# First factor of the state-space powers read by VectorE from PSUM, copied there by TensorE identity products

## The chip, the core and the metric

The program runs on one core of one Trainium2 chip. Its engines work side by side, each through its own instructions in order: TensorE (PE in the profile, with its weight loads as PEld), VectorE (DVE), ScalarE (ACT), GpSimd (POOL), and SyncE (SP), which here only issues DMA transfers. The metric is device time in microseconds (us) for one execution; lower is better.

## The reference

A trunk of two layers over 256 tokens of width 2048. Layer 0 is stick-breaking attention and a squared-ReLU MLP, layer 1 is an S5 state-space mixer with a gated unit and the same kind of MLP. What matters here are the S5 parameters, 128 groups of 64 complex states with 16 channels each:

```
mag = exp(lr * dt);  ar = mag * cos(li * dt);  ai = mag * sin(li * dt)
bbr = fr * b_re - fi * b_im;  bbi = fr * b_im + fi * b_re
h(t) = a * h(t-1) + bb * u(t)          # complex, one scan per state
y    = Re(c * h)                       # c_re, c_im
x    = x + g2 * ((relu(h @ w1) ** 2) @ w2)   # the MLP, in both layers
```

The kernel works in blocks of four time steps, so it needs b and c multiplied by the first three powers of a. These products depend on parameters alone; the change touches how the products of b are formed.

## The kernel before, in words

**The matrix products.** All large products are split in two parts for accuracy. `weights` (L124) loads a tile of 512 KB through SP (tile `w`), ScalarE rounds it to `wh` (L130), and VectorE writes the remainder `wl = w - wh` (L132). `cols_tile` then gives TensorE 24 products for it (L159 with `wl`, L160 and L161 with `wh`). `w`, `wh` and `wl` have three buffers each, so VectorE can be at most three tiles ahead of TensorE.

**The modulation vectors.** Beside these, VectorE accumulates the conditioning products (L348, L350) from tiles `adaw`, 512 KB each in four buffers, also loaded through SP. A tile of `adaw` gives two instructions. How many of them go beside one `w` tile is set by a rate in the code.

**The state-space parameters.** During the first MLP, `s5_tables` (L810) plans for each of eight groups `gi` of parameters: `s5_raws` at tick 30 + 22 gi, `s5_powers` 9 ticks later, and `s5_turns` (phase tables, GpSimd) twice; a tick is one tile of `w`. `s5_raws` issues DMAs on GpSimd's queue: b into `W` (L875), c into `C` (L879). `W` and `C` have one buffer. In `s5_powers`, TensorE transposes `C` (L895), ScalarE copies it out (L898), GpSimd forms the products of c in 13 instructions (L902 to L916), and VectorE forms the products of b in six (L920 to L925):

```
        e0, e1 = (Ec[:, c, 0:1].to_broadcast([P, 3, 8, 16]) for c in range(2))
        v.tensor_tensor(u1, e0, ar, op=OP.mult)
        v.tensor_tensor(u2, e1, ai, op=OP.mult)
        v.tensor_tensor(Ec[:, 0, 1:], u1, u2, op=OP.subtract)
        v.tensor_tensor(u1, e1, ar, op=OP.mult)
        v.tensor_tensor(u2, e0, ai, op=OP.mult)
        v.tensor_tensor(Ec[:, 1, 1:], u1, u2, op=OP.add)
        g_.dma_start(self.pw[gi], W)
```

`Ec` is the half of `W` into which the DMA of L875 has put b; `powers` holds a, a², a³. At the end GpSimd's queue sends `W` to DRAM (L926), and the next group's `s5_raws` may then overwrite it.

**What sets the order.** TensorE and GpSimd keep the order in which the code is written (`manual_schedule` in `run`). The order of VectorE, ScalarE and SP is made by a scheduler, which places an instruction where it expects its operands to be there. On the chip every engine then keeps that order, whatever is late. PSUM tiles for small results come from `mp`, four buffers in turn.

Of the kernel before, what the change touches and what calls it, by code (L numbers as in the profile page):

```python
# [16 lines left out]
P = 128  # L17
# [39 lines left out]
class Trunk:  # L57
# [824 lines left out]
    def s5_powers(self, sp, gi):  # L882
        nc, s5 = self.nc, self.s5
        v, g_ = nc.vector, nc.gpsimd
        half = lambda t, a: t[64 * a:64 * a + 64]
        qs = slice(8 * gi, 8 * gi + 8)
        bc = lambda t: t[:, qs][:, :, None].to_broadcast([P, 8, 16])
        W, C = self.raw
        Ec, Cc = W[:, 0], W[:, 1]
        CT = sp.tile([P, 2, 8, 16], F32, name="CT", bufs=1)  # L890
        pt = self.mp()
        for c in range(2):
            for b in range(2):
                o = (2 * c + b) * P
                nc.tensor.transpose(pt[:, o:o + P], C[:, c, b].rearrange("p a b -> p (a b)"), self.ident)  # L895
        for a in range(2):
            src = half(pt, a).rearrange("p (c q a e) -> p c q a e", c=2, a=2, e=16)[:, :, :, a]
            nc.scalar.activation(half(CT, a), src, AF.Copy)  # L898
        t1 = sp.tile([P, 3, 8, 16], F32, name="t1", bufs=1)
        t2 = sp.tile([P, 3, 8, 16], F32, name="t2", bufs=1)  # L900
        cr, ci, fr, fi = CT[:, 0], CT[:, 1], bc(s5["fr"]), bc(s5["fi"])
        g_.tensor_tensor(t1[:, 0], cr, fr, op=OP.mult)  # L902
        g_.tensor_tensor(t2[:, 0], ci, fi, op=OP.mult)
        g_.tensor_tensor(Cc[:, 0, 0], t1[:, 0], t2[:, 0], op=OP.subtract)
        g_.tensor_tensor(t1[:, 0], cr, fi, op=OP.mult)
        g_.tensor_tensor(t2[:, 0], ci, fr, op=OP.mult)
        g_.tensor_tensor(t1[:, 0], t1[:, 0], t2[:, 0], op=OP.add)
        g_.tensor_scalar(Cc[:, 1, 0], t1[:, 0], -1.0, None, op0=OP.mult)
        ar, ai = (s5[n][:, :, qs][:, :, :, None].to_broadcast([P, 3, 8, 16]) for n in ("ar", "ai"))
        c0, c1 = (Cc[:, c, 0:1].to_broadcast([P, 3, 8, 16]) for c in range(2))  # L910
        g_.tensor_tensor(t1, c0, ar, op=OP.mult)
        g_.tensor_tensor(t2, c1, ai, op=OP.mult)
        g_.tensor_tensor(Cc[:, 0, 1:], t1, t2, op=OP.add)
        g_.tensor_tensor(t1, c1, ar, op=OP.mult)
        g_.tensor_tensor(t2, c0, ai, op=OP.mult)
        g_.tensor_tensor(Cc[:, 1, 1:], t1, t2, op=OP.subtract)  # L916
        u1 = sp.tile([P, 3, 8, 16], F32, name="w1", bufs=1)
        u2 = sp.tile([P, 3, 8, 16], F32, name="w2", bufs=1)
        e0, e1 = (Ec[:, c, 0:1].to_broadcast([P, 3, 8, 16]) for c in range(2))
        v.tensor_tensor(u1, e0, ar, op=OP.mult)  # L920
        v.tensor_tensor(u2, e1, ai, op=OP.mult)
        v.tensor_tensor(Ec[:, 0, 1:], u1, u2, op=OP.subtract)
# [4 lines that stand above are left out]
# [300 lines left out]
```

## Time and profile before

| | us |
|---|---|
| median of 3 runs (lowest to highest) | 2525.38 (2521.66 to 2526.85) |
| the profiled execution, its own time | 2524.86 |
| span of that execution in the trace | 2523.1 |
| PE busy | 2376.2 |
| DVE busy | 1833.1 |
| ACT busy | 1208.5 |
| POOL busy | 292.2 |

The time holds 1.8 us more than the span, for what lies before the first and after the last instruction. Busy times overlap between engines and say nothing of what waits for what; for that the trace is read. The first MLP runs from about 500 to about 1390 us of the span.

### The profile page before, as it was taken

The numbers are of one execution on the slowest core, as the hardware profiler recorded it, in microseconds if no ns is written. First come the engines' busy times: TensorE is split into PE (matmuls) and PEld (weight loads), VectorE is DVE, ScalarE is ACT, GpSimd is POOL, SyncE is SP. The second block draws the span as 40 slices with busy tenths as digits, with TensorE's granted clock in tenths as the row PEclk, the third lists the DMA queues.
The fourth block names the chain that finished last, engine by engine and source line by source line (L and its number), as shares of the span: only waits on it lengthen the run. The fifth ranks groups of instructions, "written<-read, shape, count | busy, mean of one in ns | idle before, by whom it ended". The sixth has DMA issues, their size and how long they took to land.

```text
span 2523.1 us, 48416 instructions
## 1 busy us (share of the span) xinstructions
PE 2376.2 (94%) x19843; PEld 2236.4 (89%) x19843; DVE 1833.1 (73%) x2479; ACT 1208.5 (48%) x1806; POOL 292.2 (12%) x340
## 2 busy tenths in 40 slices
PE   7998999999887789788999999999999999999998
PEld 4776789899887789788999999999999999999998
DVE  5789999999787759756977897698654555554543
ACT  4534875355333334333555677444543543543543
POOL 0000100001315532345300000000000000000000
PEclk9999999999998899899999999999999999999999
DMA  9888899999987758866986884599655655655654
GB/s 335 302 300 297 282 315 316 338 308 306 310 269 266 259 180 295 271 220 205 315 291 223 289 298 139 171 325 325 218 180 184 184 184 184 184 184 184 184 188 138
DMA packets 479250, 627.28 MB, mean 249 GB/s; under 512 B 19858, under 2 KB 350004, under 8 KB 476724
## 3 DMA queue, kind: packets, MB, share of 16 engines
q1 hardware_dynamic: 474432, 606.16, 72.9%
q0 software_dynamic: 3968, 17.83, 2.2%
q8 instruction: 155, 2.54, 0.4%
q14 instruction: 67, 0.55, 0.1%
q10 hardware_dynamic: 628, 0.21, 0.0%
HBM read 607.34 MB, written 16.78 MB: 247 GB/s over the span
## 4 chain that ended last, share of the span: by engine, by line
PE 42%; DVE 5%; DMA 4%; issue 2%; ACT 1%; SPq 0%; DVEq 0%; ACTq 0%
PE acc L159 13%; PE acc L161 12%; PE acc L160 12%; DMA adaw<-in_ada_w 3%; DVE wl L132 2%; DVE adsums L350 1%; PE mp L997 1%; PE mp L1022 1%; PE mp L982 1%; PE mp L959 1%; PE mp L952 0%; DVE xT L418 0%; DVE adacc L350 0%; PE mp L967 0%; DMA W<-pw 0%
## 5 line engine op out<-in xcount | busy, mean ns | idle before, releaser
L130 ACT ACTIVATE wh<-w 128x1024 fp32r<-128x1024 f32 x736 | 777.3, 1058 | 1067.0 <-PE acc L161 617.0
L132 DVE TENSOR_TENSOR wl<-w,wh 128x1024 fp32r<-128x1024 f32 x736 | 918.6, 1249 | 417.6 <-ACT wh L130 417.2
L159 PE MATMUL acc<-hH,wl 128*128 128x258 f32 (+1 forms) x2816 | 811.9, 288 | 57.5 <-DVE wl L132 56.7
L161 PE MATMUL acc<-hH,wh 128*128 128x258 f32 (+1 forms) x2816 | 802.2, 285 | 0.0
L160 PE MATMUL acc<-hL,wh 128*128 128x258 f32 (+1 forms) x2816 | 800.9, 284 | 0.1
L159 PE MATMUL acc<-aH,wl 128*128 128x256 f32 x2048 | 583.0, 285 | 45.2 <-DVE wl L132 45.1
L159 PEld LDWEIGHTS acc<-hH,wl 128*128 128x128 f32 x2816 | 538.7, 191 | 74.2 <-DVE wl L132 55.4
L160 PE MATMUL acc<-aL,wh 128*128 128x256 f32 x2048 | 579.1, 283 | 0.0
L161 PE MATMUL acc<-aH,wh 128*128 128x256 f32 x2048 | 579.0, 283 | 0.0
L160 PEld LDWEIGHTS acc<-hL,wh 128*128 128x128 f32 x2816 | 539.6, 192 | 0.3 <-DVE hL L122 0.3
L161 PEld LDWEIGHTS acc<-hH,wh 128*128 128x128 f32 x2816 | 538.0, 191 | 0.0
L159 PEld LDWEIGHTS acc<-aH,wl 128*128 128x128 f32 x2048 | 388.5, 190 | 52.6 <-DVE wl L132 50.7
L160 PEld LDWEIGHTS acc<-aL,wh 128*128 128x128 f32 x2048 | 388.6, 190 | 0.0
L161 PEld LDWEIGHTS acc<-aH,wh 128*128 128x128 f32 x2048 | 388.5, 190 | 0.0
L350 DVE SCALAR_TENSOR_TENSOR adacc<-adaw,cond,adacc 128x512 f32<-128x512 f32 x390 | 296.7, 762 | 22.2 <-DMA adaw<-in_ada_w 18.4
L350 DVE SCALAR_TENSOR_TENSOR adsums<-adaw,cond,adsums 128x512 f32<-128x512 f32 x270 | 213.5, 792 | 22.1 <-DMA adaw<-in_ada_w 19.1
L145 PE MATMUL acc<-wh,hL 128*128 128x512 f32 x384 | 157.8, 411 | 5.8 <-ACT wh L130 3.1
L146 PE MATMUL acc<-wl,hH 128*128 128x512 f32 x384 | 154.4, 402 | 4.8 <-DVE wl L132 4.7
L147 PE MATMUL acc<-wh,hH 128*128 128x512 f32 x384 | 153.5, 400 | 0.0
L145 PEld LDWEIGHTS acc<-wh,hL 128*128 128x128 f32 x384 | 73.7, 192 | 32.4 <-issue 12.8
L146 PEld LDWEIGHTS acc<-wl,hH 128*128 128x128 f32 x384 | 73.6, 192 | 23.3 <-DVE wl L132 8.2
L147 PEld LDWEIGHTS acc<-wh,hH 128*128 128x128 f32 x384 | 73.4, 191 | 17.1
(292 smaller groups left out, 2107.9 us busy)
## 6 DMA issues: line engine op xcount, KB each, us to landing
w<-in_mlp_w SPq DMA_DIRECT2D x512, 512.0 KB, 3.8
adaw<-in_ada_w SPq DMA_DIRECT2D x384, 512.0 KB, 5.8
w<-in_sb_w_in SPq DMA_DIRECT2D x96, 512.0 KB, 5.0
w<-in_s_w_glu SPq DMA_DIRECT2D x64, 512.0 KB, 4.6
w<-in_sb_w_out SPq DMA_DIRECT2D x32, 512.0 KB, 6.0
w<-in_s_w_in SPq DMA_DIRECT2D x32, 512.0 KB, 4.9
pw<-W POOLq DMA_DIRECT2D x8, 1024.0 KB, 6.2
W<-pw SPq DMA_DIRECT2D x8, 1024.0 KB, 6.9
```

Source lines behind the costliest of these rows:

```text
L130: nc.scalar.activation(h, w, AF.Copy)
L132: nc.vector.tensor_tensor(l, w, h.bitcast(F32), op=OP.subtract)
L145: nc.tensor.matmul(o, aL(kb)[:, s], H[:, kk], start=(kb == k0), stop=False)
L146: nc.tensor.matmul(o, aH(kb)[:, s], L[:, kk], start=False, stop=False)
L147: nc.tensor.matmul(o, aH(kb)[:, s], H[:, kk], start=False, stop=(kb == k1 - 1))
L159: nc.tensor.matmul(o, L[:, kk, s], aH(kb), start=(kb == k0), stop=False)
L160: nc.tensor.matmul(o, H[:, kk, s], aL(kb), start=False, stop=False)
L161: nc.tensor.matmul(o, H[:, kk, s], aH(kb), start=False, stop=(kb == k1 - 1))
L350: nc.vector.scalar_tensor_tensor(acc, wt[:, kk], c, acc, op0=OP.mult, op1=OP.add)
L959: nc.tensor.transpose(pe[:, q * P:q * P + P], E[:, c, q].rearrange("p j a e -> p (j a e)"), self.ident)
L982: nc.tensor.matmul(pi[32 * j:32 * j + 32, 65 * q:65 * q + 65], self.ident[:, 32 * q:32 * q + 32], uw[:, 4 - j:4 - j + 257:4], start=True, ...
L997: nc.tensor.matmul(pv[:, 256 * c + 64 * q:256 * c + 64 * q + 64], VL[:, c, q], imc[:, q, 0:64], start=True, stop=True)
```

## The change

Before the transposes of `C`, TensorE multiplies the two halves of b (`Ec[:, c, 0]`, 128 x 128 each) by the identity into a tile `eb` of the pool `mp`. The four multiplications of VectorE then read their first factor from `eb` in PSUM, not from `W` in SBUF. Nothing else is edited; the two sums (L922, L925) and GpSimd's work are as before.

```
         CT = sp.tile([P, 2, 8, 16], F32, name="CT", bufs=1)
+        eb = self.mp()
+        for c in range(2):
+            nc.tensor.matmul(eb[:, c * P:c * P + P], self.ident, Ec[:, c, 0].rearrange("p q e -> p (q e)"), start=True, stop=True)
+        eb = eb[:, :2 * P].rearrange("p (c q e) -> p c q e", c=2, q=8)
         pt = self.mp()
...
-        e0, e1 = (Ec[:, c, 0:1].to_broadcast([P, 3, 8, 16]) for c in range(2))
+        e0, e1 = (eb[:, c, None].to_broadcast([P, 3, 8, 16]) for c in range(2))
         v.tensor_tensor(u1, e0, ar, op=OP.mult)
```

Lines after the insertion are numbered four higher: L895 becomes L899, L920 to L926 become L924 to L930.

The order of instructions shows what this moves. On TensorE, at the second of the eight groups (gi = 1), before; a number behind a name is that of the buffer's use, and the row of L895 stands between the products of two weight tiles, of which `wl_7758` is the second:

```order
L161 MATMUL acc_7691<-hH_4644,wh_7694 128x258
L895 MATMUL mp_7723<-ident_72,C_7394 128x128 x4
L159 MATMUL acc_7691<-hH_4644,wl_7758 128x258
L160 MATMUL acc_7691<-hL_4645,wh_7756 128x258
L161 MATMUL acc_7691<-hH_4644,wh_7756 128x258
```

And after, at the same place; the tile behind it is now called `wl_7764`:

```order
L161 MATMUL acc_7694<-hH_4644,wh_7697 128x258
L893 MATMUL mp_7726<-W_7396,ident_72 128x128 x2
L899 MATMUL mp_7729<-ident_72,C_7397 128x128 x4
L159 MATMUL acc_7694<-hH_4644,wl_7764 128x258
L160 MATMUL acc_7694<-hL_4645,wh_7762 128x258
L161 MATMUL acc_7694<-hH_4644,wh_7762 128x258
```

Two products are added ahead of the transposes at each of the eight groups; the rest of TensorE's order is the same, and GpSimd's is the same throughout.

On VectorE, the same group before; `wl_7150` is the 190th remainder tile of the program, and `wl_7758` of the rows above is the 206th:

```order
L132 TENSOR_TENSOR wl_7120<-w_7116,wh_7118 128x1024
L350 SCALAR_TENSOR_TENSOR adsums_7679<-adaw_7920,cond_113,adsums_7679 128x512 x2
L132 TENSOR_TENSOR wl_7150<-w_7146,wh_7148 128x1024
L920 TENSOR_TENSOR w1_7745<-W_7393,powers_954 128x384
L921 TENSOR_TENSOR w2_7746<-W_7393,powers_954 128x384
L350 SCALAR_TENSOR_TENSOR adsums_7679<-adaw_7994,cond_113,adsums_7679 128x512
L922 TENSOR_TENSOR W_7393<-w1_7745,w2_7746 128x384
L350 SCALAR_TENSOR_TENSOR adsums_7679<-adaw_7994,cond_113,adsums_7679 128x512
L132 TENSOR_TENSOR wl_7191<-w_7187,wh_7189 128x1024
```

And after, where the tile `wl_7764` of TensorE's rows is the 206th again and `wl_7798` the 207th:

```order
L132 TENSOR_TENSOR wl_7798<-w_7794,wh_7796 128x1024
L350 SCALAR_TENSOR_TENSOR adacc_8872<-adaw_9091,cond_113,adacc_8872 128x512
L122 TENSOR_TENSOR aL_7266<-rl_7687,aH_7265 128x512
L924 TENSOR_TENSOR w1_7751<-mp_7726,powers_954 128x384
L925 TENSOR_TENSOR w2_7752<-mp_7726,powers_954 128x384
L132 TENSOR_TENSOR wl_7828<-w_7824,wh_7826 128x1024
L926 TENSOR_TENSOR W_7396<-w1_7751,w2_7752 128x384
L350 SCALAR_TENSOR_TENSOR adacc_8872<-adaw_9091,cond_113,adacc_8872 128x512
L927 TENSOR_TENSOR w1_7751<-mp_7726,powers_954 128x384
L928 TENSOR_TENSOR w2_7752<-mp_7726,powers_954 128x384
L132 TENSOR_TENSOR wl_7870<-w_7866,wh_7868 128x1024
L929 TENSOR_TENSOR W_7396<-w1_7751,w2_7752 128x384
```

The six instructions moved 17 weight tiles later in VectorE's order, from behind the 190th to behind the 207th; they now stand two tiles ahead of TensorE, whose products for them come between the tiles 205 and 206. At the other seven groups the move is the same: at the first from behind the 168th to behind the 185th, at the last from behind the 322nd to behind the 339th, with TensorE's products always two tiles back from there. With VectorE's, SP's order of `adaw` and `w` loads was made anew in this part of the program.

## Rows read from the trace of the kernel before

**Rows 1.** Waits by line, whole kernel: total us, times, longest us.

```profile
DVE w L920 <- DMA W<-in_s_b_re: 70.2, 7, 11.9
```

**Rows 2.** Timeline of POOL, second group: start, duration, instruction.

```profile
691.64 0.91 POOL L875 DMA_DIRECT2D W<-in_s_b_re  x1
```

**Rows 3.** Timeline of DVE, second group; idle time before a row in brackets.

```profile
684.75 1.64 DVE L132 TENSOR_TENSOR wl<-w,wh 128x1024 fp32r<-128x1024 f32 x1
695.92 0.56 DVE L920 TENSOR_TENSOR w<-W,powers 128x384 f32<-128x384 f32 x1 [9.52 <-DMA W<-in_s_b_re]
...
700.35 1.64 DVE L132 TENSOR_TENSOR wl<-w,wh 128x1024 fp32r<-128x1024 f32 x1
```

**Rows 4.** Timeline of PE: its seven longest waits between 690 and 1195 us.

```profile
702.05 0.58 PE L159 MATMUL acc<-aH,wl 128*128 128x256 f32 x1 [11.49 <-DVE wl L132]
...
786.25 0.58 PE L159 MATMUL acc<-hH,wl 128*128 128x258 f32 x1 [8.88 <-DVE wl L132]
...
871.03 0.58 PE L159 MATMUL acc<-aH,wl 128*128 128x256 f32 x1 [13.81 <-DVE wl L132]
...
946.81 0.55 PE L159 MATMUL acc<-hH,wl 128*128 128x258 f32 x1 [8.38 <-DVE wl L132]
...
1033.04 0.58 PE L159 MATMUL acc<-hH,wl 128*128 128x258 f32 x1 [9.20 <-DVE wl L132]
...
1110.98 0.58 PE L159 MATMUL acc<-aH,wl 128*128 128x256 f32 x1 [10.19 <-DVE wl L132]
...
1186.21 0.58 PE L159 MATMUL acc<-hH,wl 128*128 128x258 f32 x1 [8.20 <-DVE wl L132]
```

**Rows 5.** Timeline of PE after the first of these waits.

```profile
702.42 0.41 PE L160 MATMUL acc<-aL,wh 128*128 128x256 f32 x1
702.64 0.41 PE L161 MATMUL acc<-aH,wh 128*128 128x256 f32 x1
...
705.83 0.28 PE L161 MATMUL acc<-aH,wh 128*128 128x256 f32 x1
705.95 0.28 PE L159 MATMUL acc<-aH,wl 128*128 128x256 f32 x1
```

**Rows 6.** Stretches: length, busy of PE, PEld, DVE, ACT, POOL; clock, DMA, GB/s.

```profile
410.00:690.00 280.00, 267.34 (x2143) 255.86 (x2141) 262.44 (x416) 129.62 (x176) 32.88 (x35) 1.00 0.95 316
690.00:858.00 168.00, 137.85 (x1076) 133.78 (x1068) 132.06 (x151) 65.04 (x82) 67.57 (x73) 0.93 0.83 280
...
874.00:934.00 60.00, 60.00 (x496) 59.02 (x496) 34.56 (x36) 22.59 (x23) 14.46 (x18) 0.98 0.59 190
690.00:1195.00 505.00, 416.64 (x3280) 407.36 (x3273) 355.30 (x410) 180.97 (x214) 205.86 (x232) 0.92 0.75 246
702.00:706.00 4.00, 3.95 (x19) 3.96 (x20) 3.96 (x6) 0.00 (x0) 2.24 (x3) 0.52 0.66 205
871.00:877.00 6.00, 5.97 (x30) 5.97 (x31) 4.38 (x5) 0.45 (x1) 2.23 (x3) 0.54 0.74 242
```

**Rows 7.** Timeline of PE in attention: products of two f32 operands, 128 columns.

```profile
303.29 0.38 PE L605 MATMUL mp<-sp,tri 128*128 128x128 f32 x2
303.51 0.39 PE L606 MATMUL mp<-sp,nones 128*128 128x128 f32 x2
```

**Rows 8.** Timeline of PE where it transposes `C`, second group.

```profile
749.96 0.60 PE L895 MATMUL mp<-ident,C 128*128 128x128 f32 x4
```

**Rows 9.** Timeline of DVE there: remainder tiles 207 and 208.

```profile
748.98 1.22 DVE L132 TENSOR_TENSOR wl<-w,wh 128x1024 fp32r<-128x1024 f32 x1
...
752.25 1.22 DVE L132 TENSOR_TENSOR wl<-w,wh 128x1024 fp32r<-128x1024 f32 x1
```

**Rows 10.** Single lines: duration in ns, shortest, median, longest; then first and last start.

```profile
L132 DVE TENSOR_TENSOR wl<-w,wh x736: 1193/1224/2033, 37.4 to 2510.5; 128x1024 fp32r<-128x1024 f32 x184
...
L480 DVE TENSOR_TENSOR rl<-acc,rms x56: 679/693/696, 725.8 to 2416.9; 128x514 f32<-128x514 f32 x56
...
L923 DVE TENSOR_TENSOR w<-W,powers x8: 541/918/1078, 623.9 to 1191.5; 128x384 f32<-128x384 f32 x8
```

## The prediction

> **What bounds the kernel now.** I first read the list of waits, because TensorE is busy 2376.2 of 2523.1 us and the interesting question is what the remaining 147 us are. One entry stands out that has nothing to do with TensorE: VectorE waits 70.2 us in seven pieces at L920 for the DMA that brings b into `W` [rows 1]. The timelines of the engines show why. GpSimd issues that DMA for the second group at 691.64 us [rows 2]. VectorE has finished the remainder tile of 684.75 and comes to L920, which the scheduler placed there; it stands still 9.52 us until the data lands, and its next remainder tile is written only at 700.35 [rows 3]. The wait is not one for bandwidth: the instruction simply stands too early in an order that the engine can't leave. The first of the eight groups does not wait, as seven times tell.
>
> TensorE lives on these remainder tiles. Its timeline has a wait for L132 behind each of VectorE's seven: 11.49, 8.88, 13.81, 8.38, 9.20, 10.19 and 8.20 us, together 70.15 us [rows 4]. So VectorE's wait passes on to the bounding engine in full, although the first has only 73% busy time.
>
> There is a second cost that the list of waits doesn't hold. After such a wait the products start 0.22 us apart, and 3.8 us later 0.12 us apart [rows 5]. The granted clock of that stretch is 0.52, half of full speed (1.2 of 2.4 GHz), after a stop of 11 us; after the longest stop the mean is still 0.54 over 6 us [rows 6]. Of a slow stretch, a little under half is lost. With 3.8 to 5.5 us of it per wait, I take 2 us each, 14 us for seven. The waits cost TensorE about **84 us** in all.
>
> **The change part by part.** *What it removes.* VectorE's multiplications now depend on TensorE's identity products, which the code writes 9 ticks behind `s5_raws`, so the scheduler puts them 17 weight tiles later. By then the DMA has landed long ago: TensorE transposes `C`, which came behind b through the same queue, at 749.96 [rows 8], 58 us after the issue. The wait at L920 goes, hence up to 84 us of TensorE.
>
> *What takes the place of the wait.* VectorE now can wait for `eb`. In the order it reaches L924 behind tile 207, and TensorE's products come before tile 206. In the trace of before, VectorE finishes tile 207 at 750.20 [rows 9], and the products would end some 0.4 us after 749.96: a wait of a few tenths; in lighter stretches VectorE is further ahead and waits longer, up to the buffers' end. Behind the waiting instruction is queued tile 208; TensorE has tiles 206 and 207 in hand then. A tile takes it 24 products of 0.12 us [rows 5], 2.9 us, so it needs tile 208 5.8 us later, and VectorE delivers it after two multiplications and 1.2 us of L132, some 3 us. This wait costs nothing where VectorE is no later than that.
>
> *TensorE's new work.* There is no product of `W` in the trace. The nearest row is another product of two f32 operands with 128 columns: L605 begins 0.22 us ahead of its successor [rows 7]. The transposes, 0.60 us busy for four [rows 8], bound it from below at 0.1 each. I take 0.22, as an identity product is a product, not a transpose: 16 x 0.22 = **3.5 us**, all on the path (1.6 by the lower bound).
>
> *VectorE's six instructions in their new place.* Before, they ran while TensorE stood still anyway; now they lie in the flow, beside GpSimd's 13 instructions of the same group. L923 takes 0.54 us at best and 1.08 at worst, and L132 is stretched from 1.22 to as much as 2.03 [rows 10]. The long ones lie where GpSimd computes. But L480, whose first factor is in PSUM as that of the four multiplications will be, never exceeds 0.696 us in 56 executions, from 725.8 on, in stretches where GpSimd is busy up to 41% of the time [rows 6, 10]. So I take 0.55 for the four and 0.9 for the two sums, which still read SBUF twice: 4.0 us a group.
>
> That is also where the skill speaks. The Trainium skill ("SBUF — State Buffer", section "SBUF: two separate sides") says that VectorE and GpSimd share a port pair as an exclusive lock, which a VectorE instruction with two SBUF inputs competes for. The trace agrees by the two lines just cited. By that rule the four multiplications stop competing, as the sum has it; without it they would take 0.9 each, and the eight groups 11 us of VectorE more, which would make the time some 6 us longer.
>
> What of these 4.0 us reaches TensorE depends on the stretch. In 874 to 934 TensorE is busy 60.00 of 60.00 us with VectorE at 34.56: there VectorE has room, and nothing arrives. In 410 to 690, VectorE is busy 262.44 of 280 us [rows 6]; there all may arrive. Five of the eight groups lie in such full stretches. The bounds are 0 and 5 x 4.0 = 20 us; I take half, **10 us**, since the scheduler set fewer L350 among them.
>
> *Work that used to run beside the stall.* GpSimd's phase tables overlapped VectorE's idle time. Now VectorE works through it, at stretched durations: some 9 us a group at a third more, 3 us for each of the four waits in full stretches. The bounds are 0 and 7 x 3 = 21; I take **5 us**, as the other work is not all on the path.
>
> *Loads.* From 690 to 858 the DMAs moved 280 GB/s, 47.0 MB in 168 us. Without the two waits and two slow starts in it (11.49 + 8.88 + 4 = 24.4 us) it would need 328 GB/s; the densest long stretch, 410 to 690, had 316 [rows 6], at which 47.0 MB take 149 us and only 19 us are gained. I subtract **5 us** for this. Over all of 690 to 1195 it is 246 GB/s, and 70 us less would ask 286, so elsewhere there is room.
>
> *Sum.* 84 - 3.5 - 10 - 5 - 5 = 60.5 us. A check from another side: 410 to 690 issued 2143 products in 280 us, 7.65 per us; the 3280 products of 690 to 1195 at that rate take 429 us in place of 505, a gain of 76 before the added work, 57 after the same deductions for products, VectorE and stretching. Against the profiled execution's 2524.86 the sum gives **2464 us**; that execution stands 0.5 us below the median of the runs, which makes no difference here. Behind 1195 TensorE is the bound, and what is won stays won.
>
> **The rivals.** *The full stretches keep their time* (0.17). Each stop lets the loads run up to the full buffers (three `w`, four `adaw`), so in a full stretch the loads may have been the true limit. For it speaks 95% of DMA time in 410 to 690, against it 0.83 in 690 to 858. Then only the three waits beside light stretches pay, 13.81 + 8.38 + 10.19 + 6 for the clock = 38.4, less 3.5: 2490.
>
> *Nothing of VectorE's new place arrives* (0.12). Loads and VectorE have more room than I think: 84 - 3.5 = 80.5, so 2444. The light stretches speak for it, the 94% busy VectorE of 410 to 690 against it.
>
> *The wait only changes its releaser* (0.07). VectorE comes to L924 well ahead of TensorE and stands there with the next remainder tile behind it, as it did at L920. It decides once the products come so late that the two tiles in hand run out, 5.8 us less 3, some 3 us of waiting; each further us is a us of TensorE. Eight such groups have to cost 84 / 8 = 10.5 us each, so 13 us of wait, to eat the gain; with 3.5 us of products the time is then 2528, not faster, and with a longer wait slower. Against it stand the tenths computed above. A half of this chance I give to no difference, a half to slower.
>
> The likeliest case, 2464 with a range of its own of 2450 to 2480, has 0.64.
>
> **How the numbers follow.** Beyond the unknown VectorE terms (0 to 20, 0 to 21) the range takes in both gain rivals: 2442 to 2494. It leaves out the unchanged wait and the ends of the others, under 2 in 10. A measurement of this kernel tells 0.2%, 5 us, from no change. Faster is the likeliest case with the first two rivals, 0.93; within 0.2% 0.035; slower 0.035.
>
> **What would show it.** The wait at L924 for a DMA is gone, and its wait for TensorE is under 4 us a group. TensorE's seven waits of 8 us and more are gone, and the granted clock between 690 and 1130 is at or near 1.00. The 16 products begin 0.22 us apart. L924, L925, L927 and L928 take 0.55 us beside GpSimd's work, and L926 and L929 up to 1.08. Loads reach 280 GB/s and more over the stretch. The prediction is wrong if PE still waits for L132 some 8 us a group (then on `eb`), or if waits of 1 to 3 us multiply in the full stretches beyond 20 us.

## The result and the profile after

The changed kernel takes 2468.31 us (median of 4 runs, 2465.57 to 2469.87) where the kernel before took 2524.23 in the same sessions: a ratio of 0.9777, 95% interval 0.9760 to 0.9794. That is 56 us less. The forecast was 2464, in a range of 2442 to 2494. The profiled execution took 2465.57, 1.8 us more than its span.

The head of the page of the changed kernel (span; busy time and share of each engine):

```profile
span 2463.8 us, 48495 instructions
...
PE 2373.5 (96%) x19875; PEld 2234.9 (91%) x19875; DVE 1843.6 (75%) x2479; ACT 1208.6 (49%) x1806; POOL 306.7 (12%) x340
```

TensorE is nearly as busy as before, in 59 us less. Most of what went is idle time. The list of waits of VectorE, from 480 to 1240 us, has at L924 what stood at L920 [rows 1]:

```profile
DVE adsums L350 <- DMA adaw<-in_ada_w: 25.3, 23, 5.7
...
DVE w L924 <- PE mp L893: 1.6, 2, 1.0
```

The 70.2 us are now 1.6, and TensorE, not a DMA, ends them. TensorE's own waits of 8 us and more [rows 4] are gone. Its two longest in that stretch are these (timeline of the changed kernel, idle time in brackets):

```profile
702.99 0.58 PE L159 MATMUL acc<-hH,wl 128*128 128x258 f32 x1 [4.41 <-DVE wl L132]
...
830.37 0.39 PE L159 MATMUL acc<-aH,wl 128*128 128x256 f32 x1 [3.68 <-DVE wl L132]
```

The first of them, 4.41 us, goes back to the loads: VectorE stands at L350 until a tile `adaw` lands, and its remainder tile is written only behind that (timeline of VectorE, changed kernel).

```profile
694.14 1.21 DVE L132 TENSOR_TENSOR wl<-w,wh 128x1024 fp32r<-128x1024 f32 x1
701.04 0.75 DVE L350 SCALAR_TENSOR_TENSOR adsums<-adaw,cond,adsums 128x512 f32<-128x512 f32 x1 [5.69 <-DMA adaw<-in_ada_w]
701.71 1.22 DVE L132 TENSOR_TENSOR wl<-w,wh 128x1024 fp32r<-128x1024 f32 x1
```

The second, 3.68 us, does not. VectorE works there without a break from 819.67 us on, and the tile that TensorE waits for is the first of two that take 3.64 us together beside GpSimd's products of c, where one takes 1.22 us alone (same timeline):

```profile
828.46 3.64 DVE L132 TENSOR_TENSOR wl<-w,wh 128x1024 fp32r<-128x1024 f32 x2
```

**Where the 59 us came from.** The transposes of `C` come once in each group, at the same place in TensorE's order, so they are marks for comparing two traces. Their lines give the first and the last start; before, then after:

```profile
L895 PE MATMUL mp<-ident,C x32: 270/272/273, 664.9 to 1233.1; 128*128 128x128 f32 x32
```

```profile
L899 PE MATMUL mp<-ident,C x32: 272/273/273, 662.7 to 1170.4; 128*128 128x128 f32 x32
```

568.2 us became 507.7: 60.5 us, the whole gain, lies between the marks. From mark to mark, worked out from the starts in the two timelines (the waits are those of [rows 4], one in each interval):

| interval | before, us | after, us | gained | TensorE's wait before | loads after, GB/s |
|---|---|---|---|---|---|
| 1 | 85.0 | 77.9 | 7.1 | 11.49 | 314 |
| 2 | 84.3 | 77.0 | 7.3 | 8.88 | 306 |
| 3 | 82.0 | 69.6 | 12.4 | 13.81 | 248 |
| 4 | 79.6 | 68.9 | 10.7 | 8.38 | 294 |
| 5 | 84.4 | 78.0 | 6.4 | 9.20 | 304 |
| 6 | 75.5 | 63.5 | 12.0 | 10.19 | 226 |
| 7 | 77.0 | 72.5 | 4.5 | 8.20 | 291 |

Intervals 4 and 6 gained 2.3 and 1.8 us more than their wait, about what the slow start at 1.2 GHz behind it was priced at (in interval 4 some shorter waits became less as well). The other five gained less than their wait. Against wait and slow start together, 84 us, 23.7 are missing, all in these five. Below they are called full, and interval 6 light, though the third of the five has loads of 248 GB/s only and interval 4, at 294, lacks nothing. Two stretches of the changed kernel show a light and a full interval (columns as in [rows 6]):

```profile
1034.00:1097.60 63.60, 63.60 (x539) 63.60 (x539) 37.85 (x39) 24.42 (x26) 33.12 (x36) 1.00 0.73 226
740.60:817.60 77.00, 67.86 (x539) 66.15 (x537) 69.53 (x77) 35.85 (x48) 37.43 (x36) 0.98 0.93 306
```

With the same 539 instructions, TensorE is busy throughout the light interval, and idle 9 us in the full one, where the loads are at 93% and VectorE is busy 69.5 of 77 us. What is missing can be split with two rows, from the first mark to the last, before and after (same columns):

```profile
664.90:1232.80 567.90, 476.42 (x3763) 465.39 (x3762) 410.29 (x472) 210.61 (x251) 225.62 (x252) 0.92 0.77 254
```

```profile
662.70:1170.10 507.40, 471.65 (x3791) 459.91 (x3789) 421.75 (x474) 210.61 (x252) 242.69 (x252) 0.98 0.88 285
```

TensorE's idle time fell from 91.5 to 35.8 us, by 55.7, where its seven waits had been 70.2. So 14.4 us of idle time elsewhere are new. Its busy time fell by 4.8 us although 3.1 us of new products lie between the marks; so some 8 us less were lost at the half clock of 1.2 GHz, where 14 had been forecast. The new stops bring half the clock as well: behind the wait of 4.41 us the granted clock is 0.53 over 6 us.

```profile
703.00:709.00 6.00, 6.00 (x29) 6.00 (x30) 5.79 (x11) 1.27 (x2) 0.00 (x0) 0.53 0.97 335
```

14.4 of idle time, some 6 at half the clock and 3.1 of products make up the missing 23.7. This is an estimate from one execution of each kernel, as the ends of products in a trace are modelled. What makes the new idle time was left to the experiments.

**The steps of the change.** The two products of a group begin 0.44 us ahead of the transposes, 0.22 each as forecast (timeline of TensorE, changed kernel, second group):

```profile
740.11 0.60 PE L893 MATMUL mp<-W,ident 128*128 128x128 f32 x4
740.55 0.60 PE L899 MATMUL mp<-ident,C 128*128 128x128 f32 x4
```

VectorE at the same place, with GpSimd's products of c running from 744.34 on:

```profile
743.34 0.55 DVE L924 TENSOR_TENSOR w<-mp,powers 128x384 f32<-128x384 f32 x1
...
746.69 0.54 DVE L927 TENSOR_TENSOR w<-mp,powers 128x384 f32<-128x384 f32 x1
...
748.75 0.75 DVE L929 TENSOR_TENSOR W<-w,w 128x384 f32<-128x384 f32 x1
```

And over all groups (single lines, durations in ns: shortest, median, longest):

```profile
L927 DVE TENSOR_TENSOR w<-mp,powers x8: 544/546/558, 668.9 to 1177.2; 128x384 f32<-128x384 f32 x8
```

```profile
L929 DVE TENSOR_TENSOR W<-w,w x8: 605/722/1194, 670.6 to 1179.2; 128x384 f32<-128x384 f32 x8
```

The multiplications with a factor in PSUM keep to 0.55 us; the sums, with both operands in SBUF, go up to 1.19. Before, the same multiplication took up to 1.08 [rows 10].

### The profile page after: what moved, and what is told of

It is laid out like the page before. It is cut to its first block, busy times and chain, and to the rows that moved or that the text cites. A ratio compares the mean times of both kernels' runs of the same rounds, so it can differ in the third digit from the quotient of the medians.

```text
span 2463.8 us, 48495 instructions
## 1 busy us (share of the span) xinstructions
PE 2373.5 (96%) x19875; PEld 2234.9 (91%) x19875; DVE 1843.6 (75%) x2479; ACT 1208.6 (49%) x1806; POOL 306.7 (12%) x340
## 4 chain that ended last, share of the span: by engine, by line
PE 47%; DVE 6%; DMA 6%; issue 2%; ACT 1%; SPq 0%; DVEq 0%; ACTq 0%
PE acc L159 14%; PE acc L161 14%; PE acc L160 14%; DMA adaw<-in_ada_w 5%; DVE wl L132 2%; DVE adsums L350 1%; PE mp L1001 1%; DVE adacc L350 1%; PE mp L1026 1%; PE mp L986 1%; PE mp L963 1%; DMA w<-in_mlp_w 1%; DVE xT L418 0%; PE mp L956 0%; DMA W<-pw 0%
## 5 line engine op out<-in xcount | busy, mean ns | idle before, releaser
L350 DVE SCALAR_TENSOR_TENSOR adacc<-adaw,cond,adacc 128x512 f32<-128x512 f32 x390 | 298.6, 767 | 19.4 <-DMA adaw<-in_ada_w 15.6
L350 DVE SCALAR_TENSOR_TENSOR adsums<-adaw,cond,adsums 128x512 f32<-128x512 f32 x270 | 219.3, 812 | 33.2 <-DMA adaw<-in_ada_w 29.8
L145 PEld LDWEIGHTS acc<-wh,hL 128*128 128x128 f32 x384 | 73.3, 191 | 32.3 <-issue 12.8
```

The lines of the kernel that those rows point to most:

```text
L145: nc.tensor.matmul(o, aL(kb)[:, s], H[:, kk], start=(kb == k0), stop=False)
L350: nc.vector.scalar_tensor_tensor(acc, wt[:, kk], c, acc, op0=OP.mult, op1=OP.add)
```

## The experiments

**1. The products alone.** Everything of the change but the last edit:

```
-        e0, e1 = (eb[:, c, None].to_broadcast([P, 3, 8, 16]) for c in range(2))
+        e0, e1 = (Ec[:, c, 0:1].to_broadcast([P, 3, 8, 16]) for c in range(2))
```

> The 16 identity products are issued into PSUM, but VectorE's multiplications still read b from W in SBUF, so their place in VectorE's order is that of before. Theory (the later place gives the gain): the seven waits for the DMA stay, and the products add 16 x 0.22 = 3.5 us: 2528 us against 2524 of before, between 2525 and 2531. Rival (the products themselves help, by what they do to TensorE's clock or to the course of the loads): clearly under 2520 us.

Measured: 2527.85 us against 2524.22, ratio 1.0011 (0.9999 to 1.0024). VectorE's waits hold the old entry (list of waits of this kernel, 480 to 1260 us):

```profile
DVE w L924 <- DMA W<-in_s_b_re: 66.8, 7, 13.6
```

The products gain nothing by themselves. The 3.6 us more are near the expected 3.5, though the interval reaches from no change to 6 us.

**2. The later place alone.** The kernel before, with the six instructions of VectorE kept in the order of the code:

```
+        keep = self.tc.keep_in_program_order
-        v.tensor_tensor(u1, e0, ar, op=OP.mult)
+        keep(v.tensor_tensor(u1, e0, ar, op=OP.mult))
...
```

> No identity products; VectorE reads b from W in SBUF as before, but each of the six instructions is kept behind what the code writes ahead of it on VectorE, which puts them behind remainder tile 183, 205, ..., 337, two tiles ahead of their place in the changed kernel. Theory (the later place alone gives the gain): the waits for the DMA go; against the changed kernel's 2468 it saves 3.5 us of products and pays up to 11 us of VectorE for the SBUF operands, half of which arrives: 2470 us, between 2462 and 2478. Rival (the operand in PSUM gives the gain, by taking VectorE off GpSimd's port): most of the gain is missing, 2505 us or more.

Measured: 2464.13 us against 2524.22, ratio 0.9763 (0.9747 to 0.9778). The whole gain is there without any product and without PSUM. So the place in VectorE's order is what the change is worth. (SP's order of loads was made anew here as well; experiment 8 has a kernel with a new order of loads and the six instructions in their old place, and it gains next to nothing.) TensorE and PSUM only brought the place about, because a dependency on TensorE ties the six instructions to an engine that keeps the code's order. I expected 2470, as the multiplications would be stretched by GpSimd. They are not, because they never meet it: they come two tiles sooner, ahead of GpSimd's work in all eight groups. Timelines of VectorE and of GpSimd in this kernel, second group:

```profile
739.51 0.56 DVE L922 TENSOR_TENSOR w<-W,powers 128x384 f32<-128x384 f32 x1
...
745.81 0.56 DVE L926 TENSOR_TENSOR W<-w,w 128x384 f32<-128x384 f32 x1
```

```profile
748.26 1.42 POOL L902 TENSOR_TENSOR t<-CT,fr 128x128 f32<-128x128 f32 x1 [41.33 <-ACT CT L898]
```

This kernel's median is 4 us under that of the changed one, about the price of the products; the two intervals overlap.

**3. The factor copied back to SBUF.** The changed kernel with a copy by ScalarE:

```
+        es = sp.tile([P, 64, 4], F32, name="s5tb", bufs=1)...
+        nc.scalar.activation(es, eb, AF.Copy)
-        e0, e1 = (eb[:, c, None].to_broadcast([P, 3, 8, 16]) for c in range(2))
+        e0, e1 = (es[:, c, None].to_broadcast([P, 3, 8, 16]) for c in range(2))
```

> As the changed kernel, but ScalarE copies the identity products from PSUM to SBUF and VectorE's multiplications read that copy, one tile later. The four multiplications then have two SBUF operands. If it is the operand in PSUM that keeps them at 0.55 us beside GpSimd's work, they take up to 1.08 us here, 0.9 in the mean; 8 x 4 x 0.35 = 11 us more on VectorE, of which half arrives: 2474 us. If the place alone keeps them short: 0.55 us as before and 2468 to 2469 us.

Measured: 2473.62 us against 2524.22, ratio 0.9803 (0.9784 to 0.9822); 5 us above the changed kernel, near the expected 2474, but with overlapping intervals. The lines show the operand's part apart from the time (groups by line of this kernel: busy us, mean ns):

```profile
L926 DVE TENSOR_TENSOR w<-s5tb,powers 128x384 f32<-128x384 f32 x8 | 6.0, 744 | 0.0
...
L929 DVE TENSOR_TENSOR w<-s5tb,powers 128x384 f32<-128x384 f32 x8 | 5.3, 663 | 0.1
```

The other two multiplications have the same means, 0.74 and 0.66 us. That is 0.70 us from SBUF against 0.55 from PSUM, 4.9 us in all where 11 were expected: 0.15 us each, under half of the 0.35 that I had taken. It is the direction that the port rule of the Trainium skill gives ("SBUF — State Buffer", "SBUF: two separate sides"). With half of 4.9 us arriving, the operands explain some 2.5 of the 5 us; the copies on ScalarE and a place one tile later are in them too, so that the expected time came out is in part luck.

**4. Without the six instructions.** The kernel before, with the six lines and their tiles replaced:

```
+        g_.memset(Ec[:, :, 1:], 0.0)
```

> The products of b with the powers are left out: no identity products, none of the six instructions on VectorE, and GpSimd fills their place in W with zeros. What is left is the price of the work in its new place. If VectorE's work in the full stretches is what took 10 us of the 84: 2468 - 3.5 - 10 = 2455 us. If the loads took all that is missing and VectorE's work arrives nowhere: 2468 - 3.5 = 2464.5 us.

Measured: 2461.39 us against 2524.22, ratio 0.9753 (0.9739 to 0.9768). Neither number: 6.9 us under the changed kernel, of which the products are some 3.5 (experiment 1). VectorE's six instructions in their new place cost about 3 us, and the measurement can't tell that from 0 or 6. The 10 us of the prediction are too many. GpSimd's filling with zeros is new work in this kernel.

**5. Half of VectorE's accumulations, half of their loads, and both.** On the changed kernel, from the first MLP on:

```
-                        nc.vector.scalar_tensor_tensor(acc, wt[:, kk], c, acc, op0=OP.mult, op1=OP.add)
+                        nc.vector.scalar_tensor_tensor(acc[:, :n], wt[:, kk, :n], c, acc[:, :n], op0=OP.mult, op1=OP.add)
```

with n = 256 for half the work; `wt[:, 0]` for `wt[:, kk]`, with only that half loaded, for half the loads.

> On the changed kernel, from the first MLP on, VectorE's accumulations of the conditioning products (L350) take 256 of their 512 columns; half of those sums is left out. The loads stay as they are. The question is what holds the five full groups at 69 to 78 us where a light one takes 63.6. If VectorE's work is the limit there, the stretch between the first and the last transposes of C, 507.4 us, falls by 20 us or more. If the loads are: by under 7 us.

> The mirror: on the changed kernel, from the first MLP on, a load of the conditioning weights brings 256 KB in place of 512, and VectorE's L350 reads the first half twice; half of the sum is left out. VectorE's work stays as it is. If the loads limit the full groups, the 507.4 us between the first and the last transposes of C fall by 20 us or more; if VectorE's work does, by under 7 us.

> On the changed kernel, from the first MLP on, both halvings at once: half the load of the conditioning weights and half the columns of L350; three quarters of those sums are left out. Half the work alone took 4 us off the 507.4 us between the first and the last transposes of C, half the loads alone 17.5. If the loads alone limit the full groups, this gives about 490 us, as half the loads did. If loads and VectorE are both close to the limit there, so that easing one leaves the other, it gives under 475 us.

The lines of the transposes, first half the work, then half the loads, then both (line numbers moved by the edits; the last start is that of a group's fourth transpose, so these differences are 0.3 us longer than from first to first):

```profile
L900 PE MATMUL mp<-ident,C x32: 272/273/273, 670.8 to 1174.2; 128*128 128x128 f32 x32
```

```profile
L901 PE MATMUL mp<-ident,C x32: 272/273/273, 661.5 to 1151.8; 128*128 128x128 f32 x32
```

```profile
L901 PE MATMUL mp<-ident,C x32: 272/273/273, 665.6 to 1150.8; 128*128 128x128 f32 x32
```

503.4, 490.3 and 485.2 us, against 507.7. Half the work gives 4.3 us, half the loads 17.4, both 22.5, about their sum. The first came out as expected for loads as the limit (under 7), the second just short of it (20 or more). The third lies nearer to the case of loads alone (490) than to that of two limits side by side (under 475), which did not come. So the loads appear as the main limit there and VectorE's work as a minor one.

Three things keep this from being a proof. The halvings also take away time that the kernel before had lost too, so that 22.5 is near the missing 23.7 does not make them the same time. SP's order of loads was made anew in each of the three kernels (136, 278 and 262 of its 1155 places hold another kind of load than in the changed kernel), which shifts the loads as well. And each is one profiled execution: with half the work the first mark lies 8.1 us later and the time of the whole kernel, 2467.98 us, is that of the changed one, so the 4.3 us are not clear of noise. The other two whole kernels, 2436.51 and 2427.76 us, hold what the halvings do elsewhere as well.

**6. The six instructions on GpSimd.** In the kernel before, `v.` becomes `g_.` in the six lines.

> The six instructions are handed to GpSimd, behind its 13, with no identity products; VectorE has none of them. Theory (what counts is that VectorE does not wait, and its own six cost only a few us): the waits go; 2461 us, the time without the six, plus the stretching of VectorE's work beside some 8 us more of GpSimd's per group, a third of it for five full groups, 13 us, of which half arrives: 2468 us, between 2461 and 2475. Rival (GpSimd becomes late, and its late products hold up the state-space stage): over 2480 us.

Measured: 2472.76 us against 2522.21, ratio 0.9811 (0.9798 to 0.9825). The waits go in this way too. It is 11 us above the kernel without the six, with 8.5 us more of GpSimd's work in each group beside VectorE's. I expected some 7 us from the stretching of VectorE's work, and the time is within the range given; that the stretching makes up the 11 us was not tested apart.

**7. A late place, but a later operand.** In the kernel before, GpSimd copies b behind its own products, and VectorE reads the copy:

```
+        g_.tensor_copy(es, Ec[:, :, 0])
```

> No identity products; GpSimd copies b within SBUF behind its 13 instructions, and VectorE's multiplications read the copy. They stand behind remainder tile 187, 209, ..., 341, two tiles later than in the changed kernel. If a late place in the order is enough: 2462 to 2472 us. If what counts is that the operand is there when the place comes: GpSimd's instructions end some 18 us behind the transposes, VectorE reaches its place some 6 us behind them, so it waits 10 to 12 us for GpSimd at each of eight groups, TensorE waits for L132 with it, and the gain is gone: 2520 us or more.

Measured: 2502.17 us against 2522.21, ratio 0.9919 (0.9899 to 0.9939), between the two cases. The waits of this kernel, 480 to 1260 us, first of TensorE, then of VectorE:

```profile
PE acc L159 <- DVE wl L132: 74.7, 39, 7.6
```

```profile
DVE w L922 <- POOL s5tb L920: 57.0, 8, 7.7
```

The waits are back, eight of 7 us instead of seven of 10, with GpSimd as releaser, although the place is the latest of all. Of the 60 us that the later place alone gave, 20 are left. A late place is worth what it takes off the wait; the operand has to be there when VectorE comes to it. The 10 to 12 us that I had taken were too many by 3 to 5.

**8. Loads kept even.** SP's loads of `adaw` kept in the order of the code, from the first MLP on, in three kernels:

```
-        self.nc.sync.dma_start(wt, self.i["ada_w"][layer]...)
+        d = self.nc.sync.dma_start(wt, self.i["ada_w"][layer]...)
+        if self.sums is not None:
+            self.tc.keep_in_program_order(d)
```

> As the kernel with the six instructions kept in the code's order (2464 us), and from the first MLP on SP's loads of the conditioning weights are kept in the code's order too, which puts one behind every two weight tiles, where the scheduler's order has bursts of one to one and then none. Nothing is left out. If the full groups lose time because loads and VectorE's work come in bursts: each of the seven groups falls from up to 78.5 to some 64 to 67 us, 506 us in all to some 460, and the time to some 2425 us, between 2410 and 2445. If the bursts don't matter, or late loads are needed sooner elsewhere: 2455 us or more.

> The changed kernel with the same even loads. If its products and its operand in PSUM cost what they cost with the loads in bursts: 4 us above the kernel with even loads and no products. If the two multiplications behind the wait for TensorE gain from more room on VectorE: 3.5 us, the products alone.

> The kernel before with the same even loads; its six instructions stand where they did, and wait for the DMA. Theory: each wait costs TensorE its length and the slow start, 84 us in all, and only the bursts gave 20 to 24 us of it back to nobody; with even loads the removal of the waits is worth more than the 56 to 60 us of the bursty order, some 75 to 84 us against the kernel with even loads and the six instructions in the code's order. Rival: the waits are worth the same 60 us in either order, since the missing 24 us were never lost to the waits.

| | bursts, us | even, us |
|---|---|---|
| kernel before | 2525.14 | 2522.09 |
| changed kernel | 2468.31 | 2475.29 |
| later place alone | 2464.13 | 2457.27 |

Ratios to the kernel before: 0.9982 (0.9970 to 0.9993), 0.9797 (0.9778 to 0.9815) and 0.9734 (0.9712 to 0.9755). For the later place alone the marks moved more than half as far as expected (478 us for some 460, groups of 66.4 to 69.7 for 64 to 67), and the time, 2457.27, is that of the expectation's other case (2455 or more). In the kernel before the waits stay, as its list of waits from 480 to 1260 us shows, and the new order of loads by itself gains 3 us of 2525:

```profile
DVE w L922 <- DMA W<-in_s_b_re: 66.8, 7, 11.3
```

Lines of the transposes of `C` and of the shuffles of the state-space stage, and of the last transposes of the program, for the later place alone, without and with even loads:

```profile
L895 PE MATMUL mp<-ident,C x32: 270/272/276, 665.1 to 1171.4; 128*128 128x128 f32 x32
...
L983 PE MATMUL mp<-u,ident x512: 282/297/303, 1335.5 to 1514.4; 128*32 128x65 f32 x171
...
L539 PE MATMUL mp<-ident,xT x32: 272/300/331, 2370.4 to 2460.6; 128*128 128x128 f32 x32
```

```profile
L897 PE MATMUL mp<-ident,C x32: 271/272/276, 665.4 to 1143.4; 128*128 128x128 f32 x32
...
L985 PE MATMUL mp<-u,ident x512: 282/297/304, 1301.3 to 1481.2; 128*32 128x65 f32 x171
...
L541 PE MATMUL mp<-ident,xT x32: 273/300/331, 2356.8 to 2447.0; 128*128 128x128 f32 x32
```

Even loads save 28 us between the transposes and 34 up to the state-space stage; from there to the last transposes the kernel needs 1145.7 in place of 1125.1 us, so 20.6 are given back. Stretches of both kernels at the same stage, from 200 to 500 us behind the first shuffle (columns as in [rows 6]), without and with even loads:

```profile
1535.50:1835.50 300.00, 294.00 (x2418) 289.83 (x2418) 220.88 (x292) 141.34 (x181) 0.00 (x0) 0.99 0.77 251
```

```profile
1501.30:1801.30 300.00, 282.76 (x2312) 276.58 (x2301) 244.69 (x336) 134.38 (x176) 0.00 (x0) 0.97 0.87 287
```

More loads come here, at 287 GB/s for 251, and TensorE idles 17.2 us for 6.0. Some 21 us are lost behind the first shuffle in the other two kernels with even loads as well. Whether it is the loads' arrival there or VectorE's work for them (245 us for 221) that costs the time was not tested.

Between the transposes, removing the waits is worth 550 - 478 = 72 us with even loads (kernel before with even loads: 666.5 to 1216.0) against 568 - 506 = 62 with bursts; over the whole kernel 65 against 60 (2524.22 - 2464.13). The first is near the theory's 75 to 84, the second nearer to the rival's 60, and with runs of one kernel up to 13 us apart neither settles it. That the full stretches swallowed part of what the waits had cost is supported between the marks, by some 10 us, and not shown for the whole kernel. Why the changed kernel gains only 4 us between its marks from even loads (664.1 to 1168.4) and loses in all is not settled; the scheduler made a new order for it, and the expected difference of 4 us to the later place alone, both with even loads, came out as 18.

## Why the prediction was right, point by point

**The bound.** That VectorE's wait for the DMA holds up TensorE, and that it is a matter of place and not of bandwidth, is shown by experiments 1, 2 and 7: with the place alone the gain is there, with the products alone it is not, and with a late place but a later operand two thirds of it are gone. Of the 70.2 us of waits 55.7 came back as less idle time of TensorE.

**The slow start.** 2 us for each wait was about right: intervals 4 and 6 gained 2.3 and 1.8 us beyond their wait. But the net gain between the marks is some 8 us, not 14, since the shorter stops of the changed kernel are followed by half the clock too. The forecast had no term for that.

**What takes the place of the wait.** A few tenths were forecast for a full group, 1.6 us in all were found, and TensorE's waits of 8 us and more are gone. The sign of being wrong, waits of 1 to 3 us beyond 20 us, did not come: between the marks they went from 12.8 us (8 waits) to 17.3 (12), worked out from the two timelines. From 690 to 1130 the granted clock is 0.98 and the loads run at 281 GB/s, as the signs asked. The rival in which the wait only changes its releaser did not occur here; experiment 7 shows what it would have looked like.

**TensorE's products.** 3.5 us forecast, 0.22 us each in the trace; the 3.6 us of experiment 1 agree, but can't be told from nothing.

**VectorE in its new place.** Forecast 10 us, with 5 more for other work beside GpSimd; measured some 3 us for the six instructions (experiment 4). The 5 us were not measured; half of VectorE's accumulations hold about 4.3 (experiment 5). The durations were right, 0.55 for the multiplications and 0.72 to 0.75 in the median for the sums, a little under the 0.9 assumed (the longest, 1.19, is beyond the 1.08 of the signs). The row of L480 carried less than the prediction says: of its 56 executions six lie beside GpSimd's work in the trace of before, and experiment 3 is the better evidence. The step that was off is "I take half" of the six's 20 us.

**Loads.** Forecast 5 us; by experiment 5 half of the `adaw` loads hold 17, which points to a term that is too small, though it does not measure it. 3.5 + 10 + 5 + 5 = 23.5 us were subtracted, 23.7 were missing. That the sum agrees so well is luck: the six instructions cost less than forecast, running at half the clock that stayed cost some 6 us that had no term, and the loads probably more than forecast. The figure of 316 GB/s over 280 us had been read as a rate at which such a stretch still runs well; after the change intervals 1, 2 and 5 ran at 304 to 314 GB/s and lost time. The rate alone does not decide: interval 4 ran at 294 GB/s without loss, and the wait of 3.68 us at 830.37 is one of VectorE's own work.

**The rivals.** The full stretches kept part of their time, not all: intervals 1, 2, 5 and 7 gained 4.5 to 7.3 us each, so the case of 2490, in which they gain nothing, did not come, and the case of 2444, in which nothing of the new work or the loads arrives, did not either.

## What to carry to other kernels

Where an engine waits for a DMA in an order made by a scheduler, look whether the instruction stands too early: a dependency on an engine whose order is fixed, or an explicit order, moves it, and here the explicit order gave the whole gain without the products. The move pays only if the operand is there when the engine comes to the new place. Price a long stop of TensorE with its slow start, and the stops that remain as well. And before counting a removed wait in full, look at what else in that stretch runs close to its limit, since stretches with loads at 93% gave back only part of it here.

## What the runs showed of the hardware beyond expectation

A multiplication with one factor in PSUM was never stretched: 32 of 32 took 0.540 to 0.558 us, and by the timelines 23 of these ran beside GpSimd's work for 0.3 us or more. From a copy in SBUF, one tile later and all 32 beside GpSimd's work, they took 0.544 to 0.812 us, 0.70 in the mean. Some of these, fully beside GpSimd's work, stayed at 0.55 as well. The effect is smaller than the rows of before suggested (0.92 in the median for L923 [rows 10]), where GpSimd did other work.
